# FFNs by seven products: the next chunk's gate moved ahead of a chunk's down projection

## The chip, the cores and the metric

The kernel runs on one core of one Trainium2 chip. Every time here is device time of that core in microseconds (us); a kernel's time is the median of its runs. TensorE (PE) multiplies 128-row tiles into PSUM, VectorE (DVE) and ScalarE (ACT) prepare its operands and empty its results, SyncE (SP) issues the loads.

## The reference, cut to what matters

The program is one step of a two-layer trunk for 640 tokens (512 latent, 128 context) of width 1024. A layer is FFN 1, a mixer and FFN 2, with residuals. The change touches the FFNs only:

```python
def swiglu(x, w_gate, w_up, w_down):
    return (jax.nn.silu(x @ w_gate) * (x @ w_up)) @ w_down
# per layer, for latent and context tokens with their own b, s, g:
#   x += 1/2 * g * swiglu((1 + s) * rms_norm(x) + b), D_FF = 2816 = 22 tiles of 128
```

All is float32.

## The kernel before

Of the four FFNs the first is written plainly (`ffn`); the other three run through `ffn7` (L653), here called FFN A (second of layer 0, about 846 to 1311 us of the span), B (first of layer 1, 1327 to 1782) and C (second of layer 1, 2126 to 2606). A float32 product is made of three matmuls (`product`, L584, and `mm3`, L386): each operand is split into a rounded part and a remainder, hi and lo, and hi·hi, hi·lo and lo·hi are added in PSUM. ACT rounds (a cast, L190 for weights, L821 elsewhere), DVE subtracts (L191, L822).

**Seven products.** `seven` (L596) computes two tiles of 128 hidden features for all 640 tokens with seven half-size products in place of eight. A product is 12 matmuls of 128x320. The sums of weights that it needs are made by DVE in the tile V (L616, L617, L634, L635), and split like the weights by `both` (units of 128x1024). Of PSUM a seven takes a pair of banks (products xx and zz) and a single bank (ww). It is a generator in three phases: phase 1 has two products (24 matmuls, then ACT's copy s1, L627, and DVE's add, L629), phase 2 three (36 matmuls; copies s2, L638, and s1, L641; add, L642), phase 3 two (24), after which `out` and the add at L650 read the pair. For a gate `out` ends in silu (ACT, L548); for an up it multiplies by the gate (L694, L696, L697) and `gate_done` splits the result into the tiles G, hi and lo (L821, L822).

**Chunks.** The 22 feature tiles are walked in six chunks, `SCH`: tiles 0 and 1, then five chunks of four. Tiles 0 to 3 are made plainly beforehand, 18 sevens (a gate and an up for each of nine pairs) make the other 18. A gate's or up's phase 1 stands ahead of the phase 3 of the seven before. At a chunk's end comes its down projection: for m = 0 to 7 the gated tiles times a 128-column block of w_down, two m to a load (L743), even m into a pair of banks, odd m into two single banks (`proj_parts`, L755), and DVE adds the result to the residual x (L802).

PSUM has two pairs, tags `pj` and `s2`, used in turn (`self.turn`), and three single banks `b`; raw weights, hi and lo parts have three slots each. Between the sevens of A and B, `fill` places DVE work for the modulation of the next block (L302, 1024 columns an instruction).

**What sets the order.** The statements are scheduled by a framework from the program's order, and each engine runs its own list in order. At a chunk's end the program of before runs phase 1 of the next gate (`head`, made by `begin` with `apart`, which loads the first unit alone and loads both units anew after the down projection), then the down projection, in which m = 0 and 1 stop ahead of their last two terms (`late=2`: the terms of the last up) until the first of them have been begun for both; then the gate's phase 2.

Of the kernel before, what the change touches and what calls it, by code (L numbers as in the profile page):

```python
# [10 lines left out]
F32 = mybir.dt.float32  # L11
# [13 lines left out]
T = LAT + CTX  # L25
TT = T // P
FF = 2816
NF = FF // P
FCH = ((0, 6), (6, 12), (12, 17), (17, 22))
SCH = ((0, 2), (2, 6), (6, 10), (10, 14), (14, 18), (18, 22))  # L30
HT = T // 2
# [7 lines left out]
NPL = 1 + PLAIN[-1][0] // 2  # L39
# [43 lines left out]
class Build:  # L83
# [463 lines left out]
    def silu(self, o, i):  # L547
        self.last_silu = self.nc.scalar.activation(o, i, AF.Silu)  # L548
# [44 lines left out]
            mm(o, hi[:, k], x[:, 1], start=False, stop=False, skip_group_check=True)  # L593
            mm(o, lo[:, k], x[:, 0], start=False, stop=end, skip_group_check=True)  # L594

    def seven(self, load, out, apart=False):  # L596

        nc = self.nc  # L600
        v = nc.vector
        f = lambda t: t.rearrange("p (a b) -> p a b", b=P)
        h = KD // 2 * P
        sw = [self.V[:, z * 1024:(z + 1) * 1024] for z in range(2)]
        both = lambda raw: tuple(f(t) for t in self.split(raw, 1024))
        cut = lambda w, z: tuple(t[:, 4 * z:4 * z + 4] for t in w)
        X = lambda z, s: [self.X[k + 4 * z][s] for k in range(4)]
        XT = lambda z: [self.XT[k][z] for k in range(4)]
        b2 = self.bank2()
        xx, zz, ww = b2[:, 0, :HT], b2[:, 1, :HT], self.bank()[:, :HT]  # L610
        sn = self.slot("sn", F32)
        s1, s2 = sn[:, :HT], sn[:, HT:T]
        c = [self.slot("ag", F32) for _ in range(2)]

        def first_sums():
            v.tensor_add(sw[0][:, :h], rb[:, :h], rb[:, h:])  # L616
            v.tensor_sub(sw[0][:, h:], sw[0][:, :h], ra[:, :h])  # L617
            return both(sw[0])

        ra = load(0)  # L620
        if not apart:
            rb = load(1)
        wa = both(ra)
        if not apart:
            ws = first_sums()
        self.product(xx, cut(wa, 0), X(0, 0), True)
        nc.scalar.copy(s1, xx)  # L627
        self.product(ww, cut(wa, 1), X(1, 0), True)
        v.tensor_add(c[0][:, :HT], ww, s1)  # L629
        yield  # L630
        if apart:
            ra, rb = load(0), load(1)
            ws = first_sums()
        v.tensor_sub(sw[1][:, :h], ra[:, :h], rb[:, :h])  # L634
        v.tensor_sub(sw[1][:, h:], ra[:, h:], sw[0][:, h:])  # L635
        wt = both(sw[1])
        self.product(xx, cut(ws, 1), XT(1), False)
        nc.scalar.copy(s2, xx)  # L638
        self.product(zz, cut(ws, 0), XT(0), True)
        self.product(xx, cut(wt, 0), XT(2), False)  # L640
        nc.scalar.copy(s1, xx)  # L641
        v.tensor_add(c[1][:, HT:T], zz, s1)  # L642
        wb = [self.spare(h) for z in range(2)]
        self.split2(*wb, rb[:, h:])
        wb = tuple(f(t) for t in wb)
        yield
        self.product(xx, wb, XT(3), False)
        self.product(zz, cut(wt, 1), X(1, 1), False)
        out(1, c[1], xx)
        v.tensor_add(c[0][:, HT:T], zz, s2)  # L650
        out(0, c[0], None)

    def ffn7(self, l, which, done, filler=(), half=None, cuts=CUT):  # L653

        nc, I = self.nc, self.I
        v = nc.vector
        filler = list(filler)
        self.srow = None


        calls = NF - NPL + (len(SCH) - 1) * KD // 2
        count, per = [0], len(filler)

        def fill():
            count[0] += 1
            n = len(filler) - (per - per * count[0] // calls)
            if filler and self.srow is None:
                with self.tc.issue_after(self.last_on(mybir.EngineType.SP)):
                    self.ada_rows()
            for f in filler[:n]:  # L670
                with self.tc.issue_after(self.last_on(mybir.EngineType.DVE)), self.tc.issue_after(self.last_on(mybir.EngineType.SP)):
                    f()
            del filler[:n]

        wg, wu, wd = I[f"wg{which}"], I[f"wu{which}"], I[f"wd{which}"]
        j = 0 if which == 1 else 2
        G = self.L["G"][:, j // 2]
        gsrc = self.mod[l][:, :, (3 * j + 2) * KD:(3 * j + 3) * KD]
        gated, gate_done, silu = self.gated, self.gate_done, self.silu
        cur = {}  # L680

        def pair(f, w, up, apart=False):
            def out(i, c, first):
                if not up:
                    if first is None:
                        silu(c, c)
                    else:
                        silu(c[:, :HT], first)
                        silu(c[:, HT:T], c[:, HT:T])
                    cur[f + i] = c  # L690
                    return
                tg = cur.pop(f + i)
                if first is None:
                    v.tensor_mul(c, c, tg)  # L694
                else:
                    v.tensor_mul(c[:, :HT], first, tg[:, :HT])  # L696
                    v.tensor_mul(c[:, HT:T], c[:, HT:T], tg[:, HT:T])  # L697
                gate_done(f + i, c)

            return self.seven(lambda i: self.raw(w[l, f + i], 1024), out, apart)  # L700

        def begin(ci):

            f = max(SCH[ci][0], NPL)
            g = pair(f, wg, False, True)
            next(g)
            return g

        self.finish(self.plain)
        head = None  # L710
        for ci, (f0, f1) in enumerate(SCH):
            back = None
            for f in range(max(f0, NPL), f1, 2):
                for w, up in ((wg, False), (wu, True)):
                    if head:
                        g, head = head, None
                    else:
                        g = pair(f, w, up)
                        next(g)
                    if back:  # L720
                        self.finish(back)
                    next(g)
                    back = g
                    fill()
            if back:
                self.finish(back)

            if ci + 1 < len(SCH):
                head = begin(ci + 1)
            busy = ("pj", "s2")[self.turn] if head else None  # L730
            banks = lambda m: {"pj": ("s2", None), "s2": ("pj", None)}.get(busy, (None, None))[0] if m % 2 == 0 or not busy else "b"
            if ci == 0:
                v.tensor_scalar(G, gsrc, 0.5, None, op0=ALU.mult)
            nf = f1 - f0
            last = ci == len(SCH) - 1
            held, begun = [], []
            gt = [gated[f] for f in range(f0, f1)]
            for m in range(KD):
                if m % 2 and not last:
                    fill()  # L740
                if m % 2 == 0:
                    r = self.ring("raw")[:, :2 * nf * P]
                    nc.sync.dma_start(r.rearrange("p (m a) -> p m a", m=2),  # L743
                                      wd[l, m:m + 2, :, f0:f1, :].rearrange("m p a b -> p m (a b)"))
                    w2 = [t.rearrange("p (m a b) -> p m a b", m=2, b=P) for t in self.split(r, 2 * nf * P)]
                hi, lo = (t[:, m % 2] for t in w2)
                terms = [(hi[:, k], lo[:, k], *gt[k]) for k in range(nf)]
                if last and half is not None and m >= SLATE:
                    self.proj_out(m, terms, G, 0, cuts)
                    self.sq_x(m, *cuts[0])  # L750
                    held.append((m, terms))
                    continue

                begun.append((m, self.proj_parts(m, terms, G, late=2 if m < 2 < nf else 0, tag=banks(m))))
                if m == 0:  # L755
                    if nf > 2:
                        next(begun[0][1])
                    continue
                if m == 1 and nf > 2:
                    next(begun[1][1])  # L760
                for i, g in begun:
                    self.finish(g)
                    if last:
                        done(i)
                begun = []
            self.last_load = self.last_on(mybir.EngineType.SP)
            if held:
                half(0)
                for m, terms in held:
                    self.proj_out(m, terms, G, 1, cuts)  # L770
                    self.sq_x(m, *cuts[1])
                half(1)
        assert not filler
# [1011 lines left out]
```

## Time and profile before

| | |
|---|---|
| median of 3 runs | 2600.62 us (2596.76 to 2602.01) |
| the profiled execution | 2608.11 us, its span 2606.3 us |
| PE busy | 2493.6 us, 96% of the span, 16854 matmuls |
| DVE, ACT, POOL busy | 72%, 40%, 6% |
| mean granted TensorE clock | 0.986 of full speed |
| FFNs A, B, C: PE busy of their stretch | 442.86 of 465, 435.53 of 455, 456.08 of 480 us |
| loads of gate weights | 103 of 512 KB |

A busy engine is one with an instruction in flight. Matmuls overlap: one of 320 columns is in flight for 0.31 us and the next starts 0.147 us after it. The granted clock has two levels, 1.2 and 2.4 GHz; 0.50 in a row is the lower, 1.00 the higher.

### The profile page before, as it was taken

The page shows a single profiled execution, that of the slowest core. Times are in us where ns is not written, and L with a number is a line of the kernel's source. Part 1 is how long each engine was busy: PE and PEld are TensorE (multiplying, and loading weights), DVE is VectorE, ACT ScalarE, POOL GpSimd, SP SyncE. Part 2 cuts the span into 40 slices and gives each one's busy share as a digit, 9 for nine tenths or more (in the row PEclk, how much of TensorE's full clock was granted, in tenths as well). Part 3 has the DMA queues.
Part 4 walks back from the last instruction along what each step waited for, and adds up shares of the span by engine and source line. Part 5 has one row for each costly group of instructions (what it writes and reads, how often), then busy time and mean ns, then how long its engine had stood idle before and what let it go on. Part 6 is the DMA issues. An engine that isn't in the chain of part 4 may idle for free.

```text
span 2606.3 us, 42167 instructions
## 1 busy us (share of the span) xinstructions
PE 2493.6 (96%) x16854; PEld 2405.2 (92%) x16854; DVE 1875.4 (72%) x3343; ACT 1032.4 (40%) x1918; POOL 145.8 (6%) x229
## 2 busy tenths in 40 slices
PE   9999999999999999999999999998999999999998
PEld 5999999889998899999989999997999889999998
DVE  4979688756665877777787877788567567666654
ACT  4222222354444633333463333434535455243332
POOL 0000000234000000000000000003240000000000
PEclk9999999999999999999999999999999999999999
DMA  9445444324421233333323334332264012232222
GB/s 292 168 164 194 146 167 167 105 76 127 127 73 57 86 126 116 113 128 121 97 71 132 114 113 138 114 109 62 84 166 131 31 66 66 89 106 68 80 85 76
DMA packets 151688, 296.59 MB, mean 114 GB/s; under 512 B 55108, under 2 KB 73796, under 8 KB 151492
## 3 DMA queue, kind: packets, MB, share of 16 engines
q1 hardware_dynamic: 151492, 293.90, 35.2%
q8 instruction: 132, 2.16, 0.3%
q14 instruction: 64, 0.52, 0.1%
HBM read 275.86 MB, written 18.00 MB: 113 GB/s over the span
## 4 chain that ended last, share of the span: by engine, by line
PE 80%; DVE 11%; DMA 4%; ACT 3%; issue 2%; SPq 0%; DVEq 0%; ACTq 0%
PE s L389 5%; PE s L390 5%; PE s L392 5%; PE pj L389 4%; PE pj L390 4%; PE pj L392 4%; PE pj L593 3%; PE pj L592 3%; PE s L594 3%; PE pj L594 3%; PE s L592 3%; PE s L593 3%; PE b L928 3%; PE b L592 3%; PE b L594 3%; PE b L593 3%
## 5 line engine op out<-in xcount | busy, mean ns | idle before, releaser
L190 ACT CAST wh<-raw 128x1024 fp32r<-128x1024 f32 (+4 forms) x269 | 267.8, 996 | 586.1 <-PE b L390 149.5
L191 DVE TENSOR_TENSOR wl<-raw,wh 128x1024 fp32r<-128x1024 f32 (+3 forms) x249 | 289.4, 1162 | 95.4 <-ACT wh L190 91.5
L190 ACT CAST wh<-V 128x1024 fp32r<-128x1024 f32 x108 | 113.5, 1051 | 253.4 <-PE b L390 137.6
L593 PE MATMUL b<-H,wh 128*128 128x320 f32 x600 | 186.2, 313 | 6.4 <-DVE H L822 6.1
L592 PE MATMUL b<-H,wh 128*128 128x320 f32 x600 | 185.5, 315 | 5.5 <-ACT wh L190 5.0
L594 PE MATMUL b<-H,wl 128*128 128x320 f32 x600 | 185.6, 311 | 0.0
L191 DVE TENSOR_TENSOR wl<-V,wh 128x1024 fp32r<-128x1024 f32 x108 | 132.0, 1222 | 65.0 <-ACT wh L190 65.0
L389 PE MATMUL b<-G,wh 128*128 128x256 f32 (+2 forms) x528 | 158.9, 314 | 9.3 <-ACT wh L190 9.1
L302 DVE CUSTOM_DVE_ANT_0 aw<-aw,ar,room 128x1024 f32<-128x1024 f32 x128 | 163.5, 1278 | 0.6
L302 DVE CUSTOM_DVE_ANT_0 at<-aw,ar,room 128x1024 bf16<-128x1024 f32 x128 | 163.6, 1278 | 0.1
L390 PE MATMUL b<-G,wh 128*128 128x256 f32 (+2 forms) x528 | 161.5, 310 | 0.0
L802 DVE SCALAR_TENSOR_TENSOR room<-s,room 128x512 f32<-128x512 f32 x200 | 100.8, 546 | 83.6 <-PE s L392 83.1
L390 PE MATMUL s<-G,wh 128*128 128x256 f32 x480 | 150.7, 314 | 10.6 <-DVE G L822 10.5
L389 PE MATMUL s<-G,wh 128*128 128x256 f32 x480 | 143.0, 319 | 17.5 <-DVE ag L650 12.7
L392 PE MATMUL b<-G,wl 128*128 128x256 f32 (+2 forms) x528 | 146.3, 310 | 0.0
L883 PE MATMUL pj<-wh,H 128*128 128x256 f32 (+1 forms) x416 | 122.1, 293 | 1.7 <-ACT tl L897 1.6
L884 PE MATMUL pj<-wh,H 128*128 128x256 f32 (+1 forms) x416 | 120.5, 290 | 2.3 <-DVE H L1006 2.3
L885 PE MATMUL pj<-wl,H 128*128 128x256 f32 (+1 forms) x416 | 122.5, 294 | 0.0
L593 PEld LDWEIGHTS b<-H,wh 128*128 128x128 f32 x600 | 113.8, 190 | 9.1 <-DVE H L822 8.4
L592 PEld LDWEIGHTS b<-H,wh 128*128 128x128 f32 x600 | 113.4, 190 | 7.6 <-ACT wh L190 5.7
L594 PEld LDWEIGHTS b<-H,wl 128*128 128x128 f32 x600 | 114.0, 190 | 0.0
L389 PEld LDWEIGHTS s<-G,wh 128*128 128x128 f32 x480 | 91.1, 190 | 23.7 <-DVE ag L650 16.2
(467 smaller groups left out, 7758.2 us busy)
## 6 DMA issues: line engine op xcount, KB each, us to landing
aw<-in_w_adaT SPq DMA_DIRECT2D x128, 512.0 KB
raw<-in_wg SPq DMA_DIRECT2D x103, 512.0 KB
raw<-in_wu SPq DMA_DIRECT2D x88, 512.0 KB
raw<-in_wd SPq DMA_DIRECT2D x60, 512.0 KB
raw<-in_w_in SPq DMA_DIRECT2D x24, 512.0 KB
wa<-in_w_ada SPq DMA_DIRECT2D x32, 256.0 KB
raw<-in_w_o SPq DMA_DIRECT2D x16, 512.0 KB
raw<-in_wd SPq DMA_DIRECT2D x16, 384.0 KB
```

Of the source, the lines that this page charges most:

```text
L190: self.nc.scalar.copy(hi, raw)
L191: self.eng(what).tensor_sub(lo, raw, hi.bitcast(F32))
L302: nc.vector.tensor_tensor_reduce(out=out, in0=r, in1=self.srow[g], scale=1.0, scalar=self.bada[l][:, nb:nb + 1], op0=ALU.mult, op1=ALU.add ...
L389: mm(o, wh, xh, start=first, stop=False)
L390: mm(o, wh, xl, start=False, stop=False)
L392: mm(o, wl, xh, start=False, stop=last)
L592: mm(o, hi[:, k], x[:, 0], start=first and k == 0, stop=False, skip_group_check=True)
L593: mm(o, hi[:, k], x[:, 1], start=False, stop=False, skip_group_check=True)
L594: mm(o, lo[:, k], x[:, 0], start=False, stop=end, skip_group_check=True)
L883: nc.tensor.matmul(view(i), xh, hi, start=st, stop=False, skip_group_check=True)
L884: nc.tensor.matmul(view(i), xl, hi, start=False, stop=False, skip_group_check=True)
L885: nc.tensor.matmul(view(i), xh, lo, start=False, stop=end, skip_group_check=True)
```

## The change

In `ffn7` the list of sevens becomes one queue, `todo`, and `step()` runs the next one's phase 1, the phase 3 of the seven before, and its phase 2. Before a chunk's down projection the steps go one seven further, so that the next chunk's gate has run phases 1 and 2 (five of its seven products) and the last up its phase 3. Then m = 0 and 1 of the down projection are written, whole (`late=2` stays in the last chunk only), then the gate's phase 3, then m = 2 to 7. The pair of banks that even m use is the one that the gate does not hold. The gate loads its units once: `apart` is gone, and with it 15 loads. `both` casts and subtracts in halves of 512 columns, the rounded half and then its remainder, twice, where it did 1024 at a time. The add that frees zz stands ahead of `out(1)`. Matmuls, their number and their shapes are the same.

```diff
-        both = lambda raw: tuple(f(t) for t in self.split(raw, 1024))
+        def both(raw):
+            hi, lo = self.ring("wh"), self.ring("wl")
+            for a in (0, h):
+                nc.scalar.copy(hi[:, a:a + h], raw[:, a:a + h])
+                v.tensor_sub(lo[:, a:a + h], raw[:, a:a + h], hi[:, a:a + h].bitcast(F32))
+            return f(hi), f(lo)
...
-        ra = load(0)
-        if not apart:
-            rb = load(1)
+        ra, rb = load(0), load(1)
         wa = both(ra)
...
         yield
-        if apart:
-            ra, rb = load(0), load(1)
-            ws = first_sums()
         v.tensor_sub(sw[1][:, :h], ra[:, :h], rb[:, :h])
...
         self.product(zz, cut(wt, 1), X(1, 1), False)
+        v.tensor_add(c[0][:, HT:T], zz, s2)
         out(1, c[1], xx)
-        v.tensor_add(c[0][:, HT:T], zz, s2)
         out(0, c[0], None)
...
+        todo = [(f, w, up) for f in range(NPL, NF, 2) for w, up in ((wg, False), (wu, True))]
+        back = None
+
+        def step():
+            nonlocal back
+            g = pair(*todo.pop(0))
             next(g)
-            return g
...
             if back:
                 self.finish(back)
-
-            if ci + 1 < len(SCH):
-                head = begin(ci + 1)
...
+            next(g)
+            back = g
+            fill()
+
+        for ci, (f0, f1) in enumerate(SCH):
+            while todo and (todo[0][0] < f1 or not todo[0][2]):
+                step()
+            last = ci == len(SCH) - 1
+            if last:
+                self.finish(back)
+            busy = None if last else ("pj", "s2")[self.turn]
+            other = {"pj": "s2", "s2": "pj"}.get(busy)
+            banks = lambda m: None if last else other if m % 2 == 0 else "b"
...
-                begun.append((m, self.proj_parts(m, terms, G, late=2 if m < 2 < nf else 0, tag=banks(m))))
-                if m == 0:
-                    if nf > 2:
-                        next(begun[0][1])
-                    continue
-                if m == 1 and nf > 2:
-                    next(begun[1][1])
+                begun.append((m, self.proj_parts(m, terms, G, late=2 if last and m < 2 else 0, tag=banks(m))))
+                if last and m < 2:
+                    next(begun[m][1])
+                    if m == 0:
+                        continue
                 for i, g in begun:
                     self.finish(g)
...
+                if m == 1 and not last:
+                    self.finish(back)
+                    back = None
```

The new code's line numbers are lower by 3 to 10; the prediction uses those of before.

The first place is PE's list at the end of the third chunk of FFN A (the boundary at about 1040 to 1062 us). Of before; `s2_1022` is the pair of the chunk's last up, `pj_1033` that of the next gate, `b_1039` and `b_1040` hold m = 1 of the down projection, `s2_1038` m = 0, `b_1044` a part of m = 3, `s2_1041` m = 2; `G_1029` to `G_1032` are the tiles of the last up, `G_1016` to `G_1019` those of the pair before:

```order
L594 MATMUL s2_1022_9872<-H_73,wl_78 128x320
L592 MATMUL pj_1033_10025<-H_73,wh_77 128x320 [waits DVE_49]
...
L392 MATMUL b_1039_10076<-G_1018_9819,wl_78 128x256 [waits DVE_49]
...
L592 MATMUL s2_1022_9872<-K_74,H_73 128x320 [waits DVE_49]
...
L389 MATMUL s2_1038_10062<-G_1018_9819,wh_77 128x256 [waits DVE_49]
...
L389 MATMUL b_1044_10153<-G_1018_9819,wh_77 128x256 [waits Activation_49]
...
L389 MATMUL s2_1038_10062<-G_1031_10021,wh_77 128x256 [waits Activation_49]
...
L390 MATMUL s2_1038_10062<-G_1032_10022,wh_77 128x256 [waits DVE_49]
...
L389 MATMUL s2_1041_10122<-G_1018_9819,wh_77 128x256 [waits DVE_49,PE_49]
```

And of the change (`pj_1029` is the next gate, `s2_1022` the last up, `b_1041`, `b_1042` m = 1, `s2_1038` m = 0, `s2_1043` m = 2; the last up's tiles are `G_1034` to `G_1037`):

```order
L592 MATMUL pj_1029_10023<-H_73,wh_77 128x320 [waits Activation_49]
...
L592 MATMUL s2_1022_9900<-K_74,H_73 128x320 [waits DVE_49]
...
L592 MATMUL pj_1029_10023<-K_74,wh_77 128x320 [waits Activation_49]
...
L389 MATMUL b_1041_10184<-G_1018_9845,wh_77 128x256
...
L389 MATMUL b_1042_10185<-G_1018_9845,wh_77 128x384 [waits DVE_49]
...
L389 MATMUL s2_1038_10153<-G_1018_9845,wh_77 128x256 [waits DVE_49]
...
L592 MATMUL pj_1029_10023<-K_74,wh_77 128x320 [waits Activation_49]
...
L389 MATMUL s2_1038_10153<-G_1036_10098,wh_77 128x256 [waits Activation_49]
L390 MATMUL s2_1038_10153<-G_1037_10099,wh_77 128x256 [waits DVE_49]
...
L592 MATMUL pj_1029_10023<-K_74,H_73 128x320 [waits DVE_49]
...
L389 MATMUL s2_1043_10244<-G_1018_9845,wh_77 128x256 [waits DVE_49,PE_49]
```

Before, m = 0 stood right behind the last up's phase 3 (rows `K_74,H_73` of `s2_1022`) on the same pair, with the gate's phase 1 ahead of both. Now 12 matmuls of the gate's phase 2 and 12 of m = 1 stand between that phase 3 and m = 0, and 24 more of phase 2 ahead of the first use of the last up's tiles.

The second place is PE's list behind the down projection of the same chunk. Of before (`s2_1051` is m = 6, `b_1053` a part of m = 7, `pj_1033` the gate, `s2_1056` and `b_1057` the up that follows):

```order
L389 MATMUL s2_1051_10249<-G_1018_9819,wh_77 128x256 [waits DVE_49,PE_49]
...
L389 MATMUL b_1053_10278<-G_1018_9819,wh_77 128x384 [waits DVE_49]
...
L592 MATMUL s2_1056_10362<-H_73,wh_77 128x320 [waits DVE_49,Activation_49]
...
L592 MATMUL b_1057_10363<-H_73,wh_77 128x320
...
L592 MATMUL pj_1033_10025<-K_74,wh_77 128x320 [waits Activation_49]
...
L594 MATMUL s2_1056_10362<-H_73,wl_78 128x320 [waits DVE_49]
...
L594 MATMUL b_1057_10363<-H_73,wl_78 128x320
...
L592 MATMUL pj_1033_10025<-K_74,H_73 128x320 [waits DVE_49]
```

And of the change (`b_1055` is a part of m = 7, `b_1057` and `s2_1056` the up, `b_1064` and `pj_1063` the gate after it):

```order
L389 MATMUL b_1055_10401<-G_1018_9845,wh_77 128x384 [waits DVE_49]
...
L592 MATMUL b_1057_10430<-H_73,wh_77 128x320 [waits Activation_49]
...
L592 MATMUL s2_1056_10429<-H_73,wh_77 128x320 [waits DVE_49,PE_49]
...
L592 MATMUL b_1064_10524<-H_73,wh_77 128x320 [waits Activation_49]
...
L592 MATMUL pj_1063_10523<-H_73,wh_77 128x320 [waits DVE_49,Activation_49]
...
L592 MATMUL s2_1056_10429<-K_74,wh_77 128x320 [waits Activation_49]
...
L592 MATMUL s2_1056_10429<-K_74,wh_77 128x320 [waits Activation_49]
...
L594 MATMUL b_1064_10524<-H_73,wl_78 128x320 [waits DVE_49]
```

Before, the gate's phases 2 and 3 stood between the up's phase 1 and its phase 2. Now the gate is done, and the up's phase 1 (`b_1057`, then `s2_1056` with `H_73`) is followed, after four matmuls of the next gate, by its own phase 2 (`s2_1056` with `K_74`), which waits for ACT twice.

## Rows read from the trace of the kernel before

**Rows 1.** The page's busy times: us, share of the span, instructions.

```profile
PE 2493.6 (96%) x16854; PEld 2405.2 (92%) x16854; DVE 1875.4 (72%) x3343; ACT 1032.4 (40%) x1918; POOL 145.8 (6%) x229
```

**Rows 2.** Windows: start:end, length, busy PE, PEld, DVE, ACT; ..., PEclk, DMA share.

```profile
846.00:1311.00 465.00, 442.86 (x2931) 433.71 (x2932) 365.62 (x608) 188.57 (x296) 0.00 (x0) 0.99 0.34 111
...
1062.00:1124.00 62.00, 62.00 (x421) 61.80 (x421) 48.67 (x76) 22.33 (x32) 0.00 (x0) 1.00 0.32 110
2340.00:2402.00 62.00, 62.00 (x420) 61.80 (x421) 38.27 (x59) 22.16 (x33) 0.00 (x0) 1.00 0.24 76
```

**Rows 3.** Busy time by window: twelve boundaries of chunks 1 to 4, sum.

```profile
1122.00:1145.00 23.00, 19.75 (x132) 18.82 (x131) 18.37 (x30) 8.95 (x12) 0.00 (x0) 1.00 0.44 138
...
2318.00:2341.00 23.00, 20.52 (x137) 19.58 (x136) 15.67 (x25) 8.92 (x13) 0.00 (x0) 1.00 0.36 112
...
sum 239.00, PE 204.54 PEld 193.27 DVE 178.87 ACT 89.60 POOL 0.00; mean PE 17.05 PEld 16.11 DVE 14.91 ACT 7.47 POOL 0.00
```

**Rows 4.** PE's waits at one boundary of A: us in total, times, longest.

```profile
PE s L390 <- DVE G L822: 1.2, 1, 1.2
PE s L389 <- DVE ag L650: 1.0, 1, 1.0
PE b L389 <- ACT wh L190: 0.7, 1, 0.7
PE s L389 <- DVE room L802: 0.4, 1, 0.4
```

**Rows 5.** Timeline, boundary of A's third chunk: start us, us, engine, line.

```profile
1041.21 1.04 ACT L190 CAST wh<-raw 128x1024 fp32r<-128x1024 f32 x1 [0.36 <-ACT ag L548]
1041.26 0.30 PE L593 MATMUL s<-K,wh 128*128 128x320 f32 x1
...
1042.31 0.39 PE L389 MATMUL b<-G,wh 128*128 128x256 f32 x1 [0.74 <-ACT wh L190]
...
1052.06 0.39 PE L389 MATMUL s<-G,wh 128*128 128x256 f32 x1 [0.98 <-DVE ag L650]
```

**Rows 6.** Busy time by window: boundaries of chunk 0, sum.

```profile
938.00:954.00 16.00, 13.53 (x80) 13.04 (x79) 14.56 (x24) 5.39 (x8) 0.00 (x0) 0.89 0.30 99
...
sum 35.00, PE 29.84 PEld 28.48 DVE 31.29 ACT 11.10 POOL 0.00; mean PE 9.95 PEld 9.49 DVE 10.43 ACT 3.70 POOL 0.00
```

**Rows 7.** Busy time by window: ends of the last chunk, sum.

```profile
sum 68.00, PE 60.89 PEld 57.93 DVE 36.27 ACT 27.21 POOL 0.00; mean PE 20.30 PEld 19.31 DVE 12.09 ACT 9.07 POOL 0.00
```

**Rows 8.** ACT's groups, FFN A: shapes xcount, busy us, mean ns, idle before.

```profile
L190 ACT CAST wh<-raw 128x1024 fp32r<-128x1024 f32 x45 | 47.2, 1048 | 91.3 <-PE b L390 48.6 <-issue 19.4 <-PE pj L593 9.4
...
L627 ACT COPY sn<-s 128x320 f32<-128x320 f32 x9 | 3.8, 420 | 0.0
...
L190 ACT CAST wh<-raw 128x512 fp32r<-128x512 f32 x4 | 2.5, 621 | 2.1 <-PE b L593 1.7 <-PE pj L593 0.4
```

**Rows 9.** DVE's groups of FFN A by form.

```profile
L191 DVE TENSOR_TENSOR wl<-raw,wh 128x1024 fp32r<-128x1024 f32 x45 | 54.9, 1220 | 7.5 <-ACT wh L190 7.1
...
L191 DVE TENSOR_TENSOR wl<-raw,wh 128x512 fp32r<-128x512 f32 x4 | 2.8, 690 | 3.4 <-ACT wh L190 3.4
```

**Rows 10.** Chain of waits at the same boundary: start us, us, what.

```profile
1048.61 4.29 DMA raw<-in_wg
...
1053.53 0.82 DVE ag L694
...
1056.09 1.48 DVE G L822 x2
1057.62 0.39 PE s L390
```

**Rows 11.** DVE's waits, 846:2606: us in total, times, longest.

```profile
DVE V L616 <- DMA raw<-in_wg: 21.1, 13, 4.0
```

**Rows 12.** Windows: two stretches of lower PEclk (B, C).

```profile
1691.90:1695.30 3.40, 3.40 (x13) 3.40 (x14) 2.18 (x4) 0.00 (x0) 0.00 (x0) 0.50 0.20 64
2251.70:2255.10 3.40, 3.40 (x16) 3.33 (x15) 3.01 (x5) 0.73 (x1) 0.00 (x0) 0.50 0.48 154
```

More of the change, by code (lines that the diff above doesn't have):

```diff
@@ L594, in product, with seven @@
             mm(o, lo[:, k], x[:, 0], start=False, stop=end, skip_group_check=True)
-    def seven(self, load, out, apart=False):
+    def seven(self, load, out):
         nc = self.nc
@@ L613, in seven @@
         c = [self.slot("ag", F32) for _ in range(2)]
[L615 to L618, printed above, removed]
-        ra = load(0)
-        if not apart:
-            rb = load(1)
+        ra, rb = load(0), load(1)
         wa = both(ra)
-        if not apart:
-            ws = first_sums()
+        v.tensor_add(sw[0][:, :h], rb[:, :h], rb[:, h:])
+        v.tensor_sub(sw[0][:, h:], sw[0][:, :h], ra[:, :h])
+        ws = both(sw[0])
         self.product(xx, cut(wa, 0), X(0, 0), True)
@@ L630, in seven @@
         yield
-        if apart:
-            ra, rb = load(0), load(1)
-            ws = first_sums()
         v.tensor_sub(sw[1][:, :h], ra[:, :h], rb[:, :h])
@@ L680, in ffn7, with pair @@
         cur = {}
-        def pair(f, w, up, apart=False):
+        def pair(f, w, up):
             def out(i, c, first):
@@ L698, in out @@
                 gate_done(f + i, c)
[L700 to L705, printed above, removed]
-            next(g)
-            return g
[L709 to L724, printed above, removed]
+            return self.seven(lambda i: self.raw(w[l, f + i], 1024), out)
+        self.finish(self.plain)
+        todo = [(f, w, up) for f in range(NPL, NF, 2) for w, up in ((wg, False), (wu, True))]
[3 more added lines that the diff above has]
+            g = pair(*todo.pop(0))
+            next(g)
             if back:
                 self.finish(back)
-            if ci + 1 < len(SCH):
-                head = begin(ci + 1)
-            busy = ("pj", "s2")[self.turn] if head else None
-            banks = lambda m: {"pj": ("s2", None), "s2": ("pj", None)}.get(busy, (None, None))[0] if m % 2 == 0 or not busy else "b"
+            next(g)
[10 more added lines that the diff above has]
+            banks = lambda m: None if last else other if m % 2 == 0 else "b"
             if ci == 0:
@@ L734, in ffn7 @@
             nf = f1 - f0
-            last = ci == len(SCH) - 1
             held, begun = [], []
```

## The prediction

> **What bounds the kernel now.** I read the page's busy times first: PE has work in flight for 96% of the span, DVE for 72% [rows 1]. So only PE's idle time can be won, and I looked for where it lies. Windows over the three FFNs by sevens show 442.86 of 465 us in A, and inside a chunk 62.00 of 62 us, in A as in C [rows 2]: there PE never stops. The idle time sits where one chunk's down projection meets the next chunk. Twelve windows over the boundaries of chunks 1 to 4 hold 239.00 us, of which PE is busy 204.54 [rows 3]: 34.5 us idle. Chunk 0's boundaries have 35.00 − 29.84 = 5.2 us [rows 6], the ends of the last chunks 68 − 60.89 = 7.1 [rows 7].
>
> The waits view of one boundary says what ended them: the last up's lo parts 1.2 us, the pair that the last up still holds 1.0, the cast of the down weights 0.7, a bank being emptied 0.4 [rows 4]. The timeline shows that a wait costs more than its row: the last matmul ahead of one starts at 1041.26 and the next at 1042.31, 1.05 us later, where without a wait 0.147 would have passed. That is 0.90 lost for a row of 0.74 [rows 5], since matmuls overlap. Four waits at each of twelve boundaries at 0.16 make 7.7 us more: **the boundaries of chunks 1 to 4 lose 34.5 + 7.7 = 42.2 us**. The chain of waits there runs through DVE: a reload of the gate's weights takes 4.29 us, then the multiply of the last up, then both subtractions into G (1.48) in DVE's queue, and PE starts at 1057.62 [rows 10].
>
> **The boundaries of chunks 1 to 4.** The change puts the 36 matmuls of the next gate's phase 2 and the first two terms of m = 0 and 1 between the last up's phase 3 and the places that waited. In the list of the change 24 matmuls, 3.5 us at 0.147, stand between the last up's phase 3 and m = 0. The pair is emptied by an add and a multiply that ended with the row at 1052.06, 0.98 us of wait [rows 5]; 3.5 covers it. The last up's tiles come 60 matmuls after its phase 3, 8.8 us, against waits of 1.2 and a chain of about 4 (from 1053.53 to 1057.62) [rows 4, 10]. The cast of the down weights (1.05, [rows 8]) has the last up's phase 3 and 12 matmuls more to hide behind. I take these waits as gone. The bank wait of 0.4 (L802) I keep in A and B, where even m still share one pair: 8 × (0.4 + 0.16) = 4.5, between 0 and that. Gone: 42.2 − 4.5 = 37.7.
>
> **What comes new.** In A and B, the up behind a down projection has lost its cover: before, the gate's phases 2 and 3 stood between its phase 1 and phase 2, now four matmuls do (0.6 us). Copy s1 then waits for the products' end (0.31 in flight), and, in ACT's queue, for half a cast (0.62); it takes 0.42 [rows 8]: 1.35 − 0.6 = 0.75 at most, 0.15 if no cast is in the way. I take 0.55. Copy s2 follows 12 matmuls with nothing behind them: 0.31 + 0.42 − 0.147 = 0.6. Together about 1.2, eight times: **+9.6** (bounds 6 and 11). In C, PE's list has the following gate's phase 1 in between: nothing. Where the last up's phase 3 follows 12 matmuls behind its phase 2, a half cast can hold the copy: 0.15 at each of twelve, +1.8 (0 to 4).
>
> **Chunk 0.** Its boundary in A has DVE busy 14.56 of 16 us [rows 6]; m has two terms only, 12 matmuls, and the evacuations queue behind the modulation's instructions. The moved gate brings its casts and sums into the same queue. I find waits of about 3.8 us where 2.8 stood, in A and in B: +2 (−3 to +6; −3 if the sevens cover what they cover elsewhere, +6 if each boundary loses another two subtractions' time, 2 × 1.22, [rows 9], in A and B).
>
> **The last chunk** keeps `late=2`, but m = 1 lies on banks that the last up doesn't hold, and the early terms are ordered anew: in A and B the waits for the pair and the weights go (rows of 1.0 and 0.7 like those above, [rows 4]), in part given back as longer waits for the last tiles. −3.5 of the 7.1 us [rows 7] (0 to −5). Nothing in C.
>
> **The halves.** A cast of 1024 columns takes 1048 ns, one of 512 621 [rows 8]; a subtraction 1220 against 690 [rows 9]. So a unit costs ACT at most 0.19 us more and DVE 0.16. Each seven has three units, there are 18 sevens in each of three FFNs, 162 units: 31 us of ACT and 26 of DVE, in a kernel where ACT is idle 60% and DVE 28% [rows 1]. Inside a chunk PE is full while DVE is busy 48.67 of 62 [rows 2]; the chunk's dozen units take under 2 of the 13 us that are free. I price them at 0; the cover is DVE's slack, and a rival below takes it away. The Trainium skill, "Perfetto Trace Analysis", section Optimizing Scalar/DVE Operations, gives a fixed cost of an instruction in SBUF of about 60 ns on DVE and 93 on ACT, and says to group work where an engine is saturated and to break it up where it is not and others wait. By that page the halves would cost DVE an estimated 162 × 0.06 = 10 us and ACT 15, less than the rows' 26 and 31; neither changes the sum while DVE has slack.
>
> **Loads and the rest.** Fifteen loads of 512 KB fall away from SP's queue. DVE waited 13 times for gate loads at L616, 21.1 us in all [rows 11], and one such load heads the chain above; that gain is already in the waits counted as gone. DMA is busy a third of the time [rows 2], so nothing more. The add ahead of `out(1)` frees the pair no sooner as both must end: 0. PE's count is the same.
>
> **Clock.** Two stretches at boundaries of this kind run at 0.50, the lower level, 3.40 us each [rows 12]; each costs about half its length. They stand behind idle stretches that go; I take one of the two: −1.7 (0 to −3.4).
>
> **Sum:** −37.7 + 9.6 + 1.8 + 2 − 3.5 − 1.7 = −29.5, about **−30 us**. Against the profiled execution's 2608.11 that is 2578; the median of the runs is 2600.62, 7.5 lower, and the forecast is stated there: **2570 us**. With all terms at their ends it would be 2552 to 2583.
>
> **The rivals.**
> 1. *Every up behind a down projection stalls in full, in C and behind chunk 0 too*: the copies wait for a half cast and DVE's add for a half subtraction, 1.2 + 0.69 [rows 9] = 1.9 us, 15 times, 28 where I counted 9.6: **2589 us**. For it: PE's list in A and B. Against: C's list has cover.
> 2. *DVE becomes the bound in A and B*, by the rule of grouping: 108 halved units at 0.16 = 17 us [rows 9] come out in the time: **2587 us**. For it: 14.56 of 16 at chunk 0 [rows 6], 18.37 of 23 at a later boundary [rows 3]. Against: 13 us free in each 62 inside a chunk [rows 2]. The page named above states that rule.
> 3. *Slower, by late loads.* The raw slots are three. Behind the change the up's second unit can be loaded only when m = 4's weights are split, late in the down projection, and DVE's sum of it stands in its queue ahead of the evacuations. If it lands late, DVE blocks, the banks stay full and PE stops, as in the chain where 4.29 us of loading head the waits [rows 10]. From issue to need I count about 5.5 us, so it decides where a landing takes over 7.5: at 15 boundaries with the longest wait seen, 4.0 [rows 11], 60 us come on: 2600.6 − 30 + 60 = **2631 us**. Against: the load read there took 4.29.
> 4. *The change doesn't do what it says*: the waits move from these instructions to others of equal length, as the last chunk's do in part: **2600 us**.
>
> **How the numbers follow.** Forecast 0.64, rival 1 0.13, rival 2 0.10, rival 3 0.08, rival 4 0.05. The range 2552 to 2594 takes in the forecast's ends and the first two rivals. A measurement here tells about 0.2%, 5.2 us, from no change: faster has the forecast and rivals 1 and 2, less a little for their upper ends, 0.86; the same 0.06; slower 0.08.
>
> **What would show it.** In the changed profile the windows over the boundaries should have PE near full; the rows of the waits for L650 and L822 at the first matmuls of the down projection should be gone; new ones of 0.5 to 0.6 us should stand at the up's L592 behind the down projection in A and B, waiting for ACT's copies; L190's casts of 512 near 620 ns, and 88 gate loads. I am wrong if DVE waits for `raw<-in_wu` behind m = 4 (rival 3), if DVE's busy share in A rises to 90% with PE waiting for wl (rival 2), or if PE's idle time at the boundaries stays near 35 us (rival 4).

## The result, and the profile after

| | before | the change |
|---|---|---|
| median | 2601.32 us (4 runs, 2596.76 to 2606.75) | 2566.56 us (4 runs, 2560.18 to 2569.47) |
| ratio to before | | 0.9863, 95% interval 0.9845 to 0.9881 |
| profiled execution | 2608.11 us | 2560.18 us |
| mean granted clock there | 0.986 | 0.989 |

The change makes the kernel 34.8 us faster; 30 were forecast. The profiled executions lie 47.9 us apart, since the one of before is above its other runs and the one of after the quickest of its four. From start to start, each stretch with the mixer's last projections ahead of its FFN, A and B together took 976.6 us and now 947.1 (−29.5), C 496.9 and now 483.0 (−13.9). The other 4.5 us lie in stages that the change doesn't touch.

The page's busy times after the change, which answer to [rows 1]:

```profile
PE 2476.1 (97%) x16854; PEld 2394.2 (94%) x16854; DVE 1879.1 (73%) x3505; ACT 1052.9 (41%) x2081; POOL 145.9 (6%) x229
```

PE has the same 16854 matmuls, DVE 162 instructions more and ACT 163. Busy time by window after the change (start:end, length, then busy PE, PEld, DVE, ACT): FFN A (the part that [rows 2] has at 846 to 1311), the boundaries of the third and fourth chunk of A and of the third of C, and the stretch behind the down projection of A's third chunk:

```profile
845.00:1296.00 451.00, 440.90 (x2936) 433.63 (x2936) 367.89 (x664) 194.39 (x350) 0.00 (x0) 0.99 0.33 109
1041.00:1064.00 23.00, 23.00 (x159) 23.00 (x158) 15.22 (x24) 9.02 (x15) 0.00 (x0) 1.00 0.42 138
1120.00:1143.00 23.00, 23.00 (x159) 23.00 (x158) 15.20 (x24) 9.03 (x15) 0.00 (x0) 1.00 0.46 153
2364.00:2387.00 23.00, 23.00 (x159) 22.82 (x158) 13.44 (x21) 9.43 (x14) 0.00 (x0) 1.00 0.28 93
1081.00:1090.00 9.00, 8.22 (x54) 7.67 (x53) 9.00 (x18) 3.13 (x7) 0.00 (x0) 1.00 0.00 0
```

In [rows 3] such a boundary had 19.75 of 23 us, now 23.00 of 23: it is as full as the inside of a chunk. PE's idle time in FFN A fell from 22.1 us to 10.1. At the third chunk of A what is left stands behind the down projection, 8.22 of 9. PE's waits from 846 us to the end, which takes in the three FFNs and the mixer between B and C; before (us in total, times, longest):

```profile
PE s L389 <- DVE ag L650: 12.7, 14, 1.3
...
PE s L390 <- DVE G L822: 10.5, 9, 1.2
PE b L389 <- ACT wh L190: 9.1, 11, 1.0
PE s L594 <- DVE wl L191: 6.8, 10, 2.3
...
PE s L389 <- ACT G L821: 2.8, 4, 0.8
...
PE s L389 <- DVE room L802: 1.6, 6, 0.4
```

and after:

```profile
PE s L592 <- DVE room L793: 2.4, 2, 1.2
PE s L592 <- DVE ag L639: 2.3, 6, 1.1
...
PE pj L592 <- ACT wh L609: 2.1, 8, 0.3
PE s L592 <- ACT sn L635: 2.1, 4, 0.5
```

None of the six groups of before is left: 43.5 us of rows went, and the four largest new groups make 8.9 us. (The ends of the last chunks, where PE waits for G on `pj`, went from 2.1 to 3.8 us.) The bank wait (L802 before, L793 now) is gone from the matmuls of the down projection too; the 2.4 us that remain are the ups behind chunk 0. Two of the new waits, behind the third chunk of A:

```profile
1085.19 0.41 PE L592 MATMUL pj<-H,wh 128*128 128x320 f32 x1 [0.27 <-ACT wh L609]
1085.44 0.30 PE L593 MATMUL pj<-H,wh 128*128 128x320 f32 x1
...
1088.05 0.42 PE L592 MATMUL s<-K,wh 128*128 128x320 f32 x1 [0.52 <-ACT sn L635]
```

The first is the next gate's product, held by the first half of its cast; the last is the up's phase 2, held by copy s2. The row between shows that the matmul behind a wait is late too: it starts 0.25 us after the one that waited, where 0.147 is usual. With that 0.1 and the 0.16 of the prediction a wait costs about 0.26 us beyond its row.

The halved forms in FFN A, ACT and then DVE (shapes, count, busy us, mean ns, idle before):

```profile
L609 ACT CAST wh<-V 128x512 fp32r<-128x512 f32 x72 | 44.7, 622 | 97.5 <-PE s L390 32.4 <-PE s L593 22.8 <-PE b L390 19.6
```

```profile
L610 DVE TENSOR_TENSOR wl<-V,wh 128x512 fp32r<-128x512 f32 x72 | 49.5, 690 | 15.0 <-ACT wh L609 14.8
```

Twice 622 ns against 1048 [rows 8], twice 690 against 1220 [rows 9]: by the rows the price per unit is what was reckoned, 0.2 and 0.16 us. In busy time it is less. Run e1 below is the change with whole units, and its page has

```profile
PE 2482.8 (95%) x16854; PEld 2396.2 (92%) x16854; DVE 1866.4 (72%) x3343; ACT 1028.4 (40%) x1918; POOL 145.7 (6%) x229
```

Beside it the halves cost DVE 12.7 us and ACT 24.5 (in e2 beside before 1.7 and 17.0), where the prediction had 26 and 31 from the rows. Where DVE's queue is full, the next instruction starts before the row ahead of it ends: 0.60 us after the start of a half of 0.69, and 1.13 after that of a whole subtraction of 1.22.

### The profile page after: what moved, and what is told of

Same layout as the page of the kernel before. It is cut to its first block, busy times and chain, and to the rows that moved or that the text cites. A ratio compares the mean times of both kernels' runs of the same rounds, so it can differ in the third digit from the quotient of the medians.

```text
span 2558.4 us, 42599 instructions
## 1 busy us (share of the span) xinstructions
PE 2476.1 (97%) x16854; PEld 2394.2 (94%) x16854; DVE 1879.1 (73%) x3505; ACT 1052.9 (41%) x2081; POOL 145.9 (6%) x229
## 4 chain that ended last, share of the span: by engine, by line
PE 86%; DVE 8%; ACT 2%; DMA 2%; issue 1%; SPq 0%; DVEq 0%; ACTq 0%
PE s L389 6%; PE s L390 6%; PE s L392 6%; PE s L592 4%; PE s L593 4%; PE pj L592 4%; PE pj L389 4%; PE pj L390 4%; PE s L594 4%; PE pj L392 4%; PE pj L594 4%; PE pj L593 4%; PE b L594 3%; PE b L592 3%; PE b L392 3%; PE b L593 3%
## 5 line engine op out<-in xcount | busy, mean ns | idle before, releaser
L190 ACT CAST wh<-raw 128x1024 fp32r<-128x1024 f32 (+4 forms) x215 | 211.3, 984 | 439.9 <-PE s L390 118.7
L191 DVE TENSOR_TENSOR wl<-raw,wh 128x1024 fp32r<-128x1024 f32 (+3 forms) x195 | 223.6, 1147 | 116.9 <-ACT wh L190 114.4
L609 ACT CAST wh<-V 128x512 fp32r<-128x512 f32 x216 | 134.0, 622 | 298.5 <-PE s L390 99.5
L610 DVE TENSOR_TENSOR wl<-V,wh 128x512 fp32r<-128x512 f32 x216 | 148.2, 688 | 59.1 <-ACT wh L609 58.3
L793 DVE SCALAR_TENSOR_TENSOR room<-s,room 128x512 f32<-128x512 f32 x200 | 100.9, 547 | 93.9 <-PE s L392 93.5
L390 PE MATMUL s<-G,wh 128*128 128x256 f32 x480 | 148.4, 309 | 0.0
L389 PE MATMUL s<-G,wh 128*128 128x256 f32 x480 | 138.1, 310 | 0.0
L592 PEld LDWEIGHTS b<-H,wh 128*128 128x128 f32 x600 | 113.5, 191 | 10.8 <-ACT wh L190 5.7
L392 PE MATMUL s<-G,wl 128*128 128x256 f32 x480 | 110.4, 309 | 0.0
```

The costliest lines, as they stand in the source:

```text
L190: self.nc.scalar.copy(hi, raw)
L191: self.eng(what).tensor_sub(lo, raw, hi.bitcast(F32))
L389: mm(o, wh, xh, start=first, stop=False)
L390: mm(o, wh, xl, start=False, stop=False)
L392: mm(o, wl, xh, start=False, stop=last)
L592: mm(o, hi[:, k], x[:, 0], start=first and k == 0, stop=False, skip_group_check=True)
```

## The experiments

Ratios are to the kernel before on the same chip, with 95% intervals. In all of them the framework schedules anew, so an edit can also change PE's order. It did so in every run but e12, so a difference in time is that of the edit together with the order that came of it.

| run | what it is | median us | ratio |
|---|---|---|---|
| e1 | the change, whole units | 2603.01 | 1.0006 [0.9992, 1.002] |
| e2 | before, halved units | 2593.19 | 0.9963 [0.9949, 0.9978] |
| e3 | the change, gate's phases 2 and 3 behind m = 1 | 2600.24 | 0.9996 [0.9986, 1.0007] |
| e4 | the change, 15 loads back | 2563.49 | 0.985 [0.9835, 0.9865] |
| e5 | the change, m = 6 in the freed pair | 2553.16 | 0.9812 [0.9793, 0.9831] |
| e8 | the change, halves for loaded units only | 2569.12 | 0.9871 [0.9855, 0.9888] |
| e9 | the change, halves for sums only | 2584.07 | 0.993 [0.9911, 0.9949] |
| e10 | e5, no modulation work in chunk 0's down projection | 2548.22 | 0.9797 [0.9783, 0.9811] |
| e11 | e5, halves for loaded units only | 2572.41 | 0.9882 [0.9869, 0.9895] |
| e12 | the change again | 2565.78 | 0.9855 [0.984, 0.9869] |
| e13 | e8, DVE's subtraction whole | 2585.55 | 0.9939 [0.9925, 0.9953] |

**e1: whole units.**

```diff
-        def both(raw):
...
+        both = lambda raw: tuple(f(t) for t in self.split(raw, 1024))
```

> The change, with whole units of 1024 columns again instead of halves. Theory C (the next gate's phase 2 covers the boundary, the halves are worth nearly nothing): PE's list still has phase 2 between the last up's phase 3 and the first terms of m = 0, 14 matmuls instead of 24, so a few tenths per boundary return: ratio to before 0.986 to 0.990, 2566 to 2574 us. Rival H (the halves make the casts punctual and earn much of the gain): over half of the 35 us is lost, 2585 us or more. Casts of 1024 near 1048 ns.

The whole gain was gone, as rival H said and more. PE's waits from 846 us on:

```profile
PE pj L592 <- ACT wh L190: 15.7, 16, 1.0
PE s L592 <- ACT wh L190: 9.9, 10, 1.0
...
PE pj L592 <- ACT ag L548: 5.2, 5, 1.3
```

and two of them in the timeline, each with its cast:

```profile
1037.96 1.05 ACT L190 CAST wh<-V 128x1024 fp32r<-128x1024 f32 x1 [1.14 <-PE pj L593]
...
1039.06 0.41 PE L592 MATMUL s<-K,wh 128*128 128x320 f32 x1 [0.99 <-ACT wh L190]
```

```profile
1089.83 1.04 ACT L190 CAST wh<-raw 128x1024 fp32r<-128x1024 f32 x1 [2.54 <-PE s L593]
...
1090.93 0.41 PE L592 MATMUL pj<-H,wh 128*128 128x320 f32 x1 [1.03 <-ACT wh L190]
```

These casts waited for a PE read (their releasers are PE's matmuls), and PE then stood through all of each: 1.0 us a row, 26 rows in the first two groups, 25.6 us of the 36 that came back, and about 32 with 0.26 us more for each. The waits at the down projection itself stayed away; the new ones stand ahead of it (1039.06 is the last up's phase 2) and behind it (1090.93). As I read these rows, a boundary with the gate moved ahead makes its units in close succession, each goes into a slot that PE has just left, and PE wants it at once. PE's list changed as well: the last up's phase 3 moved behind the first 12 matmuls of the gate's phase 2; how much of the loss is due to that, e1 can't tell. So the prediction's sum for the halves, 0, was right for their price and wrong for their worth: without them the time that the cover gains is lost again in waits for casts.

**e2: only the halves.** The edit of `both` from the change, made in the kernel before.

> The kernel before with nothing but the halved units. Theory C: the boundary waits for the pair (1.0), the up's tiles (1.2) and the down weights' cast (0.7) stay, 2601 us within 5. Rival H: 2585 us or less. Rival D (halving costs DVE and ACT a fixed time each and DVE is the bound in FFNs A and B): slower by up to 17 us, 2618 us.

About 9 us, between theory C and rival H. By themselves the halves are worth a quarter of the gain; rival D (DVE as the bound) is refuted, this kernel has the same 324 half subtractions. The wait for the down weights' cast fell from 9.1 us to 5.2; the pair and the up's tiles still held PE:

```profile
PE s L389 <- DVE ag L655: 9.2, 11, 1.0
...
PE s L390 <- DVE G L827: 7.2, 7, 1.2
...
PE b L389 <- ACT wh L190: 5.2, 5, 1.0
```

**e3: without the cover.**

```diff
-            next(g)
+            if not ahead:
+                next(g)
...
                 if m == 1 and not last:
-                    self.finish(back)
+                    with self.tc.issue_after(self.last_on(mybir.EngineType.PE)):
+                        self.finish(back)
```

> The change, but of the next chunk's gate only phase 1 runs ahead of the down projection; its phases 2 and 3 are issued behind m = 1, with single loads and halves kept. Theory C: the cover is gone, so the waits for the pair behind the last up's phase 3 (1.0 and 0.16) and for the up's tiles (about 1.2 and 0.16 or more, 16 matmuls behind that phase 3) return at twelve boundaries, 12 times 2.5 = 30 us: 2597 us (2585 to 2605). Rival L (the gain comes from the 15 loads that are gone, whose landing held DVE's queue ahead of the up's tiles): 2566 to 2575 us.

2600 us where theory C said 2597, and rival L 2566 to 2575. The size is right, the waits are others than expected:

```profile
PE s L389 <- ACT wh L190: 12.3, 12, 1.0
...
PE pj L592 <- ACT sn L635: 7.7, 15, 0.5
...
PE s L392 <- DVE wl L191: 4.6, 12, 0.4
```

At twelve boundaries PE stops for the cast of the down weights, which waits for its slot until the last up's phase 3 is through, and not for the pair:

```profile
1049.02 1.04 ACT L190 CAST wh<-raw 128x1024 fp32r<-128x1024 f32 x1 [1.14 <-PE s L593]
...
1050.12 0.39 PE L389 MATMUL s<-G,wh 128*128 128x256 f32 x1 [1.04 <-ACT wh L190]
...
1060.34 0.42 PE L592 MATMUL pj<-K,wh 128*128 128x320 f32 x1 [0.52 <-ACT sn L635]
```

The last row is the gate's own phase 2: with nothing between its products it waits for copy s2, 0.52 us, fifteen times. That wait comes of e3's own order and not of the down projection left bare: of the three groups, 16.9 us are the missing cover and 7.7 are this.

**e4: the loads again.** `if again: ra = load(0)` behind phase 1 of the gates that run ahead.

> The change, with the next chunk's gates loading their first unit a second time ahead of phase 2 (15 loads of 512 KB more, as many as before the change). Theory C: the second load is issued early and lands under 36 matmuls; little changes, 2566 to 2572 us. Rival L: DVE's first difference of weights waits for the load (3 to 4 us) with the up's subtractions queued behind it, PE loses 1 us or more at each of 15 boundaries: 2580 to 2595 us.

No loss: 0.985 against 0.9863 and, beside later runs, 0.9855 for the change. The page shows the loads, and DVE's waits from 846 us on the time that they cost:

```profile
raw<-in_wg SPq DMA_DIRECT2D x103, 512.0 KB
```

```profile
DVE V L623 <- DMA raw<-in_wg: 3.8, 3, 1.5
...
DVE V L633 <- DMA raw<-in_wg: 1.1, 3, 0.6
```

Before, 21.1 us of DVE's time went to such waits at L616 alone [rows 11]; with the same 103 loads it is 3.8 (4.0 in the change). So the load as such costs nothing. That its late place, ahead of the up's multiply in DVE's queue, cost time before is read from [rows 10] and was not tried by itself.

**e5: another pair for m = 6.**

```diff
-            banks = lambda m: None if last else other if m % 2 == 0 else "b"
+            banks = lambda m: None if last else "b" if m % 2 else busy if m == 6 else other
```

> The change, with m = 6 of the down projection in the pair of banks that the gate has freed, so that the up behind the down projection finds its own pair free. Theory P (the new waits behind the down projection, 0.54 at every boundary of A and B and 0.79 at every other one by start to start, come from the up's first product standing behind its second, because m = 6 still holds the pair): the first product goes ahead, its copy s1 is covered by the second, and 4 to 6 us go: ratio to before 0.984 to 0.985, 2560 to 2563 us. Rival Q (the wait is the next gate's first cast, which waits for its slot, whatever the pair): 2565 to 2569 us, ratio 0.986.

Theory P in direction, and about twice its size: 13 us by the medians, 10.8 by the FFNs of the profiles. A and B together took 939.8 us (947.1 in the change, 946.5 in e12), C 479.5 (483.0 and 483.2). Behind the down projection of A's third chunk the 0.27 and 0.52 became

```profile
PE s L592 <- ACT sn L635: 0.2, 1, 0.2
```

since PE's list now has the up's first product ahead of its second, and copy s1 under it. In C the wait for the add (L639) at the up's phase 3 went as well, 0.5 us at each boundary from start to start; I hadn't expected anything there.

**e8, e9, e13: which halves.** e8 keeps `both` for `ra` and splits the sums whole, e9 the reverse; e13 is e8 with one subtraction of 1024 columns behind the two casts.

> The change, with halves for the loaded units (the first unit of a seven) only; the two units of sums whole. After the run with whole units, in which the whole gain was lost and PE waited 26 us for casts: theory S (both kinds count, each about half): 2580 to 2590 us. Rival W (only the first unit counts, since a seven's first product needs only its first half): 2564 to 2570 us. Rival V (only the sums count): 2597 to 2605 us.

> The change, with halves for the two units of sums only; the loaded first unit whole. Theory S: 2580 to 2590 us. Rival W: 2597 to 2605 us. Rival V: 2564 to 2570 us.

> The change, with only ACT's cast of the first unit in halves; DVE subtracts all 1024 columns at once, and the sums are whole. Theory A (the waits that whole units brought back are all for the cast: PE can begin when half of the rounded unit is there): as with halves of the first unit, 2566 to 2572 us. Rival B (the remainders count as much, since the third matmul of each tile needs them): 2580 us or more.

In the change's own order of banks rival W holds for e8: the loaded unit's halves give 0.9871, nearly all (A and B as in the change; C 7 us longer in the profile, about half of that by two more stretches at the lower clock). But e9 keeps half the gain where W left nothing, so the parts don't add. e13 falls with rival B, though its trace doesn't show B's mechanism: A and B took 960.3 us against 946.1 in e8, and the waits that came are for copies, none for the remainders of sums:

```profile
PE s L592 <- ACT sn L636: 4.6, 9, 0.5
...
PE s L592 <- ACT sn L628: 3.4, 7, 0.7
...
PE pj L594 <- DVE wl L610: 0.8, 1, 0.8
```

PE's list in e13 is another than in e8 within A already. So e13 is no verdict on cast against remainder.

**e11 and e10: on top of e5.** e11 is e8's edit in e5; e10 takes `fill()` out of the down projection of chunk 0 (`if m % 2 and not last and ci:`).

> The version with m = 6 in the freed pair, with halves for the loaded first unit only. If the halves of the sums earn nothing, 2553 us within 4, as they did not in the change itself (2569 against 2567); if the new order of banks makes them matter, 2560 us or more.

> The version with m = 6 in the freed pair, and besides the modulation's work is no longer placed between the m of chunk 0's down projection (it goes to the other places). Theory F (chunk 0 in A and B stops PE because a remainder of the weights stands in DVE's queue behind evacuations and 1024-column instructions of the modulation): the two waits of 2.5 us go, 4 to 5 us gained on the 2553 us: 2548 us. Rival G (DVE's evacuations alone hold it): 2552 to 2555 us.

e11 refutes that the sums' halves earn nothing: with the better pair they are worth 19 us. e10 came out at the 2548 us that theory F gave, but its interval overlaps e5's, so the times alone don't tell it from e5. The waits do. At the end of chunk 0 of A, and over A and B, e5 had

```profile
941.00:957.00 16.00, 13.37 (x89) 12.85 (x88) 15.70 (x32) 6.00 (x12) 0.00 (x0) 1.00 0.29 99
```

```profile
PE s L594 <- DVE wl L610: 4.1, 2, 2.3
```

and e10

```profile
943.00:959.00 16.00, 15.03 (x101) 14.58 (x100) 15.70 (x32) 5.95 (x11) 0.00 (x0) 1.00 0.41 130
```

```profile
PE pj L389 <- ACT ag L548: 1.6, 2, 1.0
```

The two waits for a remainder, one in A and one in B, are gone as theory F said; in their places stand two shorter ones, for silu ahead of m = 6. It is the quickest version here, 56 us under before in its batch.

**e12: the change again.**

> The change itself once more, beside the others on one chip: ratio to before 0.9863 within 0.002, 2566 us.

0.9855 and 0.9863 agree.

## Why the prediction was right, point by point

**The boundaries of chunks 1 to 4** (−42.2, of which 4.5 kept: −37.7). The waits are gone and the windows full. They were worth more than reckoned: from start to start the twelve windows of [rows 3] lost 47.5 us, not 42.2, since a wait costs about 0.26 us beyond its row and not 0.16; the matmul behind the one that waited is 0.1 late as well. That the cover of phase 2 does it is shown by e3, if not to its full size: without the cover 34 us return, but part of that is the gate's phase 2 in its new place. The term kept, the bank wait, was not there: 24 matmuls of the gate's phase 3 now stand ahead of m = 2.

**What comes new** (+9.6, and +1.8). The places were right, the names half so. In A and B the first wait is for the next gate's cast, not for copy s1, 0.54 us from start to start at all eight boundaries; copy s2 (0.52 in its row, 0.79 from start to start; I had 0.6) holds PE only at every second one: 8 × 0.54 + 4 × 0.79 = 7.5. The up's phase 3 costs 0.26 and not 0.15 at eight of the twelve, 0.54 at a ninth and nothing at three, 2.6. "In C nothing" was wrong by 0.5 at each of four, 2.0.

**Chunk 0** (+2) and **the last chunk** (−3.5). From start to start chunk 0 lost about 1 us more over the three FFNs. That the modulation's work in DVE's queue holds it is shown by e10 for the order of banks of e5; in the change itself, whose waits there are for banks and casts, it is inferred. The last chunk gained 1.1 and 1.4 us in A and B and lost 1.2 in C, where phase 3 stands right behind phase 2: −1.3.

**Clock** (−1.7). Both stretches of [rows 12] are gone, and over the three FFNs nine stretches of 3.41 us at the lower level became six, worth about 5 us by half their length. But that holds for these two profiles only. The profile of before ran at a mean granted clock of 0.986, its 45 executions beside the experiments at 0.989 on the average, the four of the change at 0.985 to 0.989. Beside e5 the kernel before took 2594.89 us at 0.991 and 2611.27 at 0.985. So the executions show no gain by the clock.

**Sum from start to start:** −47.5 + 7.5 + 2.6 + 2 + 1 − 1.3 = −36 for the waits. With 5 by the clock that is 41 of the 43.4 us between the FFNs of the two profiles; the waits alone lie near the 34.8 us between the medians. That the forecast's −30 came so near is in part luck: its largest term, the boundaries, was 10 us too small (47.5 against 37.7), and the last chunk (−1.3 against −3.5) and the clock (none against −1.7) made up for 4 of it.

**The halves** (0) are the step that failed. Their price is no more than reckoned, and DVE's slack covers it: rival 2 would have cost 17 us, and e2 gained 9 instead. But I put them down as neutral, and they are a condition: e1 has the cover and gains nothing. The walk through PE's list that the forecast rests on was made with halves in it and so held their worth without naming it. The other sentence of the Trainium skill, "Perfetto Trace Analysis", section Optimizing Scalar/DVE Operations, that breaking up work on an engine that isn't saturated may let others go on sooner, agrees with e1 and e2 here, 36 and 9 us.

**Loads** (0): right, by e4. **Rival 3** (late loads of the up's second unit): DVE's waits for such loads are short, as in the `raw<-in_wu` row of the change, so it had no case:

```profile
DVE V L623 <- DMA raw<-in_wu: 3.3, 6, 1.2
```

**Still open:** whether whole units hurt by their length (1.05 us to 0.62) or because a slot is freed in halves; both are in e1's rows. A fourth slot for the parts would tell; it wasn't tried. Open too is how much of e1's loss, and of e8's, e9's and e11's, is the order that the framework made: no run has whole units in the order of the change.

## What to carry to other kernels

A stage boundary is filled by work of the next stage that needs none of the results still in flight. Here it took both: the work moved ahead, and its operands made in pieces that its first product could start on. Count the buffers that the moved work takes from the stage that it passes: here the pair of banks for m = 6 was worth another 11 to 13 us. An edit priced at nothing still has to be taken out alone in a trial: what this forecast had wrong in its mechanism lay in a term of 0.

## What was not expected of the hardware

Two sizes were: a wait of PE costs 0.26 us beyond its row, as the matmul behind the one that waited is late too, and halving DVE's subtractions costs at most half of what their rows say (12.7 us or less for 26). The larger surprise was in the program: parts that don't add up. Cover alone gives 0, halves alone 9 us, both 35.
